# One more chunk pair on seven products in each feed-forward block of a decoder layer

## The chip, the cores and the metric

The kernel runs on one core of one Trainium2 chip. The metric is the device time of one execution in microseconds. A core has five engines, each with its own instruction queue that runs in order: TensorE (PE in the profile; its weight loads are PEld), VectorE (DVE), ScalarE (ACT), GpSimd (POOL) and SyncE (SP, which here only issues transfers). They meet through semaphores: an instruction that waits holds everything behind it on its engine. Weights come from device memory by DMA into on-chip memory (SBUF); matmul results go to accumulation banks (PSUM), of which this kernel uses eight, three named `acc`, three `mm` and two `tr`.

## What is computed

One decoder layer on 256 tokens of width 2048, in float32: a feed-forward (SwiGLU, inner width 5632), a mixer of sliding-window attention and a gated linear recurrence, cross-attention into a fixed memory, a second feed-forward, and a last norm. Cut to what matters here:

```python
def rms_norm(x, g):
    y = x * lax.rsqrt(jnp.mean(x * x, axis=-1, keepdims=True) + NORM_EPS)
    return y * g

def swiglu(h, w_gate, w_up, w_down):
    return (jax.nn.silu(h @ w_gate) * (h @ w_up)) @ w_down

x = x + 0.5 * swiglu(rms_norm(x, ffn1_norm), ffn1_w_gate, ffn1_w_up, ffn1_w_down)
x = gated_parallel_mixer(x, ...)
x = memory_cross_attention(x, mem, ...)
x = x + 0.5 * swiglu(rms_norm(x, ffn2_norm), ffn2_w_gate, ffn2_w_up, ffn2_w_down)
return rms_norm(x, final_norm)
```

## The kernel before

**Precision.** Every large operand is kept as two parts, hi (a rounded copy, made by ScalarE) and lo (operand less hi, made by VectorE). A product of a 128-row chunk of x with a 128 x 512 piece of weights is then three matmuls that add up in one bank: hi by hi, hi by lo, lo by hi (`times`, lines 397 to 399). For weights, `split_unit` makes hi (line 324) and lo (line 325) of two chunks at a time, 128 x 1024 numbers. hi and lo have three buffers each, so a split waits until TensorE is done with the piece three splits back.

**Feed-forward.** The inner width is cut into eleven column blocks j of 512, in groups of 4, 4 and 3. A block needs x by gate and x by up for both halves t of the tokens (128 each) over all sixteen chunks of x. After a group the product with the down weights follows. Block j = 0 takes plain products, gate and then up (`product`). The other ten (`product_pair`) go over eight chunk pairs q, 0 to 7. A plain pair takes eight products of a chunk (gate and up, two halves, two chunks), 24 matmuls. A pair in `SEVEN` takes seven, 21 matmuls, by the scheme of fast 2 x 2 matrix multiplication: with p1 to p7 from sums of x and sums of weights, all four results come out of seven products. For the sums of weights, `sums` adds four 128 x 512 pieces on VectorE (lines 335 to 338) into two tiles, ta and tb, and splits them into thi (line 340) and tlo (line 341), which have one buffer. For the sums of x, `combinations` makes, once for each feed-forward, four combinations for a pair in `SEVEN`, and two for a plain pair ahead of the last pair in `SEVEN` (`EARLY`); the adds run on GpSimd (lines 423 to 435), the cast chi on ScalarE (438) and clo on VectorE (439). Partial results stay in banks: p1, p3 and p5 in mm, p2 and p4 in acc, p6 and p7 in the two tr banks until the last pair in `SEVEN`, where VectorE folds them together (lines 497 to 501). From then on p2 to p5 collect the four results, which lines 513 to 521 turn into silu(gate) * up at the block's end.

Each block's result hb is transposed on TensorE through the tr banks (`feat`, line 534) and split into h (lines 539, 540) for the down product. These steps are a background generator, `transposed`, advanced by ticks between products.

**Weights.** In the feed-forwards a transfer brings 1 MB, four chunks of one weight ("wide", tile raw2, four buffers); a buffer comes free when VectorE has made the last lo from it. The second feed-forward's first four transfers still are of the narrow kind (tile raw). The wide tiles lie in the pool f2, whose memory the mixer's pool used before; the first transfer into each waits for the mixer's last use of that memory.

**Order.** The program text gives an order of issue; on each engine the final order is made by the framework's scheduler, from its own estimates. Work put in the order ahead of something late holds all behind it.

**Start of the second feed-forward.** `combinations` starts with the feed-forward; its adds, casts and splits run beside block j = 0, whose Silu is at line 607. GpSimd also brings x back from device memory there (line 1360).

Of the kernel before, what the change touches and what calls it, by code (L numbers as in the profile page):

```python
# [34 lines left out]
AHEAD, LOADED = 2, 4  # L35


SEVEN = (1, 3)
EARLY = tuple(q for q in range(max(SEVEN)) if q not in SEVEN)


# [87 lines left out]
def decoder_layer(ctx: ExitStack, tc: tile.TileContext, a: dict, out: bass.AP):  # L129
# [276 lines left out]
                k + i == 0, k + i == nk - 1,  # L406
            )

    def combinations(sp, x: Act):


        n = 4 * len(SEVEN) + 2 * len(EARLY)
        parts = [sp.tile([P, n, P], F32R, tag="c" + e, name="c" + e) for e in ("hi", "lo")]
        c = {"parts": parts, "at": {}, "done": False}

        def work():
            o = 0
            for q in range(max(SEVEN) + 1):
                while not {2 * q, 2 * q + 1} <= x.done:
                    yield  # L420
                v = sp.tile([P, 2, 2, P], F32, tag="u", name="u", bufs=2)
                f = sp.tile([P, 4, P], F32, tag="u", name="u", bufs=2)
                pool.tensor_tensor(
                    v[:].rearrange("p k t n -> p k (t n)"), f32(x.at(0, 2 * q, 2)),
                    f32(x.at(1, 2 * q, 2)), ALU.add,
                )
                if q in SEVEN:
                    n = 4
                    pool.tensor_tensor(f[:, 0], v[:, 0, 1], v[:, 1, 1], ALU.add)
                    pool.tensor_tensor(f[:, 1], f[:, 0], v[:, 0, 0], ALU.subtract)  # L430
                    pool.tensor_tensor(f[:, 2], v[:, 0, 0], v[:, 0, 1], ALU.subtract)
                    pool.tensor_tensor(f[:, 3], v[:, 1, 0], f[:, 1], ALU.subtract)
                else:
                    n = 2
                    pool.tensor_tensor(f[:, :2], v[:, :, 0], v[:, :, 1], ALU.subtract)
                yield from idle(3)
                s = slice(o, o + n)
                act.copy(parts[0][:, s], f[:, :n])
                dve.tensor_tensor(parts[1][:, s], f[:, :n], f32(parts[0][:, s]), ALU.subtract)
                c["at"][q] = o  # L440
                o += n
                yield
            c["done"] = True

        bg.spawn("mem", work())
        return c

    def product_pair(sp, x: Act, c, r, w):

        pw, _, nk, _, n = plan[at["product"]]
        assert pw[0].tensor is w.tensor
        at["product"] += 1
        b, begun = {}, set()
        hb = sp.tile([P, 2, 512], F32, tag="hb", name="hb", bufs=2)
        u2, u3 = (sp.tile([P, 512], F32, tag="u", name="u", bufs=2) for _ in range(2))
        late = nk // KU - 1  # L460

        def add(to, x_, w_, last):
            if to not in b:
                b[to] = {"p1": mm, "p3": mm, "p5": mm, "p2": acc, "p4": acc}.get(to, tr)()
            times(
                b[to][:], x_, w_, to not in begun, last, skip_group_check=True,
            )
            begun.add(to)

        def of_x(t, k):  # L470
            return [x.at(p, k)[:, t * P : (t + 1) * P] for p in range(2)]

        def of_c(q, i):
            return [p[:, c["at"][q] + i, :] for p in c["parts"]]

        def of_w(parts_, i):
            return [p[:, i, :] for p in parts_]

        for q in range(nk // KU):
            k = KU * q  # L480
            last = q == late
            if q in SEVEN:
                bg.until(lambda: c["done"])
                g, u, s = next_item()
                end = q == max(SEVEN)
                seven = (
                    ("p1", of_x(0, k), of_w(g, 0), end), ("p2", of_x(0, k + 1), of_w(g, 1), False),
                    ("p3", of_c(q, 3), of_w(u, 1), False), ("p5", of_c(q, 0), of_w(s, 0), end),
                    ("p7", of_c(q, 2), of_w(s, 1), end), ("p6", of_c(q, 1), of_w(s, 2), end),
                    ("p4", of_x(1, k + 1), of_w(s, 3), False),  # L490
                )
                for i, p in enumerate(seven):
                    add(*p)
                    if i % 2:
                        bg.tick()
                    if end and i == 1:
                        act.copy(hb[:, 0], b["p1"][:])
                if end:
                    dve.tensor_tensor(u2[:], b["p6"][:], hb[:, 0], ALU.add)
                    dve.tensor_tensor(u3[:], b["p7"][:], u2[:], ALU.add)  # L500
                    dve.tensor_tensor(u2[:], b["p5"][:], u2[:], ALU.add)
                continue
            g, u = next_item()
            for to, t, wt in (("p2", 0, g), ("p4", 1, g), ("p3", 0, u), ("p5", 1, u)):
                for i in range(KU):
                    off = to == "p3" and q in EARLY
                    add(
                        to, of_c(q, i) if off else of_x(t, k + i), of_w(wt, i),
                        last and i == KU - 1,
                    )  # L510
                if last:
                    if to == "p2":
                        dve.tensor_tensor(hb[:, 0], b["p2"][:], hb[:, 0], ALU.add)
                        act.activation(hb[:, 0], hb[:, 0], AF.Silu, scale=r[0])
                    elif to == "p4":
                        dve.tensor_tensor(hb[:, 1], b["p4"][:], u3[:], ALU.add)
                        act.activation(hb[:, 1], hb[:, 1], AF.Silu, scale=r[1])
                    else:
                        t, v = (0, u2) if to == "p3" else (1, u3)
                        dve.tensor_tensor(v[:], b[to][:], v[:], ALU.add)  # L520
                        dve.scalar_tensor_tensor(
                            hb[:, t], v[:], r[t], hb[:, t], ALU.mult, ALU.mult
                        )
                bg.tick()
        return hb
# [18 lines left out]
    class Norm:  # L544
        def __init__(self, gain, x=None):
            self.gain = gain
            self.ss = stat.tile([P, 2, 4], F32, tag="ss", name="ss")
            self.x = x or Act(
                [xtp.tile([P, KD, T], F32R, tag="xhi", name="xhi")],
                [xtp.tile([P, KD, T], F32R, tag="xlo", name="xlo")], KD,  # L550
            )
# [32 lines left out]


    def feed_forward(sp, x, norm: Norm, wg, wu, wd, done, begin_last=lambda: None, last=False):
        c = combinations(sp, norm.x)
        for gi, (j0, nj) in enumerate(GROUPS):
            h = Act(
                [sp.tile([P, 16, T], F32R, tag="hhi", name="hhi")],  # L590
                [sp.tile([P, 16, T], F32R, tag="hlo", name="hlo")], 16,
            )

            def transposed(hb, c):
                for q in range(2):
                    split(h, c + 2 * q, 2, feat(hb, [2 * q * P, (2 * q + 1) * P]))
                    yield

            for j in range(j0, j0 + nj):
                if j > 0:  # L600
                    hb = product_pair(sp, norm.x, c, norm.r, wg)
                    bg.spawn("feat", transposed(hb, 4 * (j - j0)))
                    continue
                pg = product(norm.x, wg)
                hb = sp.tile([P, 2, 512], F32, tag="hb", name="hb", bufs=2)
                for t in range(2):
                    act.activation(hb[:, t, :], pg[t][:], AF.Silu, scale=norm.r[t])
                pu = product(norm.x, wu)
                for t in range(2):
                    dve.scalar_tensor_tensor(  # L610
                        hb[:, t, :], pu[t][:], norm.r[t], hb[:, t, :], ALU.mult, ALU.mult
                    )
                bg.spawn("feat", transposed(hb, 4 * (j - j0)))
            if gi == len(GROUPS) - 1:
                begin_last()
            for n in range(4):
                end = gi == len(GROUPS) - 1
                pd = product(h, wd, skew=last and end and n == 3)
                for t in range(2):
                    xs = x[:, t, n * 512 : (n + 1) * 512]  # L620
                    dve.scalar_tensor_tensor(xs, pd[t][:], 0.5, xs, ALU.mult, ALU.add)
                if end:
                    done(n)
# [796 lines left out]
```

## Time and profile before

| | |
|---|---|
| three runs, median (lowest to highest) | 2307.45 us (2306.52 to 2311.22) |
| the profiled execution, its time | 2307.24 us |
| its span on the core, mean granted TensorE clock | 2305.5 us, 0.997 |
| first feed-forward, from first matmul to last column block's down product | about 8 to 740 us |
| second feed-forward | about 1573 to 2300 us |
| copy of p1 to copy of p1 in neighbouring blocks | 43.18 us |
| DMA, mean rate over the span | 188 GB/s |

A row of the profile names engine, source line, operation, output and inputs, shape and count, then busy time and mean duration; the idle time before it and what ended that stand last. Durations of neighbouring matmuls overlap, so what a matmul costs is read from the distance between the starts. In the table of stretches the columns are busy time and count by engine (PE, PEld, DVE, ACT, POOL), granted clock, share of DMA and GB/s.

### The profile page before, as it was taken

The page shows a single profiled execution, that of the slowest core. Times are in us where ns is not written, and L with a number is a line of the kernel's source. Part 1 is how long each engine was busy: PE and PEld are TensorE (multiplying, and loading weights), DVE is VectorE, ACT ScalarE, POOL GpSimd, SP SyncE. Part 2 cuts the span into 40 slices and gives each one's busy share as a digit, 9 for nine tenths or more (in the row PEclk, how much of TensorE's full clock was granted, in tenths as well). Part 3 has the DMA queues.
Part 4 walks back from the last instruction along what each step waited for, and adds up shares of the span by engine and source line. Part 5 has one row for each costly group of instructions (what it writes and reads, how often), then busy time and mean ns, then how long its engine had stood idle before and what let it go on. Part 6 is the DMA issues. An engine that isn't in the chain of part 4 may idle for free.

```text
span 2305.5 us, 27706 instructions
## 1 busy us (share of the span) xinstructions
PE 2279.0 (99%) x10751; PEld 1867.7 (81%) x10751; DVE 1511.0 (66%) x1784; ACT 1143.8 (50%) x1534; POOL 159.1 (7%) x221
## 2 busy tenths in 40 slices
PE   9999999999999999999999999998999999999998
PEld 7888888888888877778888888887888888888886
DVE  6875677657865477895444466556875677756865
ACT  6544445434545467444344446555554454534544
POOL 4000000000000000201220030003000000000001
PEclk9999999999999999999999999999999999999999
DMA  7555565565564544676423576647565565555553
GB/s 252 188 200 190 193 201 194 190 199 192 201 233 143 163 139 138 193 227 210 141 85 101 166 262 224 191 164 245 183 207 195 183 205 197 197 187 201 200 201 128
DMA packets 219236, 432.73 MB, mean 188 GB/s; under 512 B 14139, under 2 KB 16416, under 8 KB 219104
## 3 DMA queue, kind: packets, MB, share of 16 engines
q1 hardware_dynamic: 210432, 404.78, 52.7%
q0 software_dynamic: 8208, 25.39, 3.4%
q8 instruction: 84, 1.38, 0.2%
q10 hardware_dynamic: 464, 0.79, 0.1%
q14 instruction: 48, 0.39, 0.0%
HBM read 417.56 MB, written 13.11 MB: 187 GB/s over the span
## 4 chain that ended last, share of the span: by engine, by line
PE 90%; issue 4%; DVE 2%; ACT 1%; DMA 1%; POOL 1%; SPq 0%; POOLq 0%; ACTq 0%; DVEq 0%
PE acc L397 21%; PE acc L398 21%; PE acc L399 21%; PE mm L399 6%; PE mm L397 6%; PE mm L398 6%; PE tr L534 2%; PE mm L1119 1%; PE tr L399 1%; PE tr L397 1%; PE tr L398 1%; DVE lo L325 1%; PE tr L1088 1%; ACT s L762 0%; ACT hi L324 0%
## 5 line engine op out<-in xcount | busy, mean ns | idle before, releaser
L325 DVE TENSOR_TENSOR lo<-raw,hi 128x1024 fp32r<-128x1024 f32 (+1 forms) x770 | 918.3, 1198 | 652.3 <-ACT hi L324 648.4
L324 ACT CAST hi<-raw 128x1024 fp32r<-128x1024 f32 (+1 forms) x770 | 784.4, 1025 | 930.1 <-PE acc L399 713.5
L397 PE MATMUL acc<-hi,xhi 128*128 128x512 f32 (+1 forms) x1256 | 500.1, 399 | 7.8 <-ACT hi L324 2.9
L398 PE MATMUL acc<-lo,xhi 128*128 128x512 f32 (+1 forms) x1256 | 491.6, 391 | 3.5 <-DVE lo L325 3.4
L399 PE MATMUL acc<-hi,xlo 128*128 128x512 f32 (+1 forms) x1256 | 490.3, 391 | 1.2 <-DVE xlo L561 1.2
L397 PEld LDWEIGHTS acc<-hi,xhi 128*128 128x128 f32 x1256 | 236.5, 188 | 60.6 <-issue 5.1
L398 PEld LDWEIGHTS acc<-lo,xhi 128*128 128x128 f32 x1256 | 237.0, 189 | 53.7 <-DVE lo L325 5.5
L399 PEld LDWEIGHTS acc<-hi,xlo 128*128 128x128 f32 x1256 | 236.5, 188 | 50.3 <-DVE xlo L561 2.5
L397 PE MATMUL acc<-hi,hhi 128*128 128x512 f32 x704 | 275.0, 391 | 0.0
L399 PE MATMUL acc<-hi,hlo 128*128 128x512 f32 x704 | 274.6, 390 | 0.0
L398 PE MATMUL acc<-lo,hhi 128*128 128x512 f32 x704 | 274.6, 390 | 0.0
L398 PE MATMUL mm<-lo,xhi 128*128 128x512 f32 x440 | 171.2, 389 | 0.0
L399 PE MATMUL mm<-hi,xlo 128*128 128x512 f32 x440 | 171.2, 389 | 0.0
L397 PE MATMUL mm<-hi,xhi 128*128 128x512 f32 x440 | 171.2, 389 | 0.0
L398 PEld LDWEIGHTS acc<-lo,hhi 128*128 128x128 f32 x704 | 132.2, 188 | 27.1
L399 PEld LDWEIGHTS acc<-hi,hlo 128*128 128x128 f32 x704 | 132.2, 188 | 26.9
L397 PEld LDWEIGHTS acc<-hi,hhi 128*128 128x128 f32 x704 | 132.2, 188 | 26.8
L341 DVE TENSOR_TENSOR tlo<-raw,thi 128x1024 fp32r<-128x1024 f32 x80 | 95.9, 1219 | 19.9 <-ACT thi L340 19.9
L398 PEld LDWEIGHTS mm<-lo,xhi 128*128 128x128 f32 x440 | 82.6, 188 | 17.3
L397 PEld LDWEIGHTS mm<-hi,xhi 128*128 128x128 f32 x440 | 82.6, 188 | 17.2
L399 PEld LDWEIGHTS mm<-hi,xlo 128*128 128x128 f32 x440 | 82.6, 188 | 17.2
L340 ACT CAST thi<-raw 128x1024 fp32r<-128x1024 f32 x80 | 82.0, 1050 | 28.1 <-PE acc L399 27.9
(347 smaller groups left out, 2618.2 us busy)
## 6 DMA issues: line engine op xcount, KB each, us to landing
raw<-in_ffn_w_up_dram SPq DMA_DIRECT2D x88, 1024.0 KB, 5.1
raw<-in_ffn_w_down_dram SPq DMA_DIRECT2D x88, 1024.0 KB, 5.1
raw<-in_ffn_w_gate_dram SPq DMA_DIRECT2D x84, 1024.0 KB, 5.1
raw<-in_w_in_dram SPq DMA_DIRECT2D x136, 512.0 KB, 3.5
raw<-in_w_out_dram SPq DMA_DIRECT2D x32, 512.0 KB, 4.7
raw<-in_w_proj_attn_dram SPq DMA_DIRECT2D x16, 512.0 KB, 3.5
raw<-in_w_proj_rwkv_dram SPq DMA_DIRECT2D x16, 512.0 KB, 6.4
raw<-in_w_cross_kv_dram SPq DMA_DIRECT2D x16, 512.0 KB, 3.6
```

What stands on the lines that cost most here:

```text
L324: act.copy(hi[:, s], raw[:, s])
L325: dve.tensor_tensor(lo[:, s], raw[:, s], f32(hi[:, s]), ALU.subtract)
L340: act.copy(hi[:, 2 * i : 2 * i + 2], t[:])
L341: dve.tensor_tensor(lo[:, 2 * i : 2 * i + 2], t[:], f32(hi[:, 2 * i : 2 * i + 2]), ALU.subtract)
L397: pe.matmul(o, xh, hi, start=first, stop=False, **how)
L398: pe.matmul(o, xh, lo, start=False, stop=False, **how)
L399: pe.matmul(o, xl, hi, start=False, stop=last, **how)
L534: pe.transpose(b[:, o : o + P], tok[:, t, col : col + P], ident[:])
L1088: pe.matmul(b[e][:, m * P : (m + 1) * P], x1[r, j, cs_], x2[r, j, cs_], start=True, stop=True,)
L1119: pe.matmul(vb[:, o : o + P][:, r], lhs(e), rhs[:, r], start=first and e == 0, stop=True, **ek,)
```

## The change

Three edits, and what follows from them:

- `SEVEN` goes from pairs 1 and 3 to pairs 0, 2 and 4, so three of eight pairs take seven products; `EARLY` becomes 1 and 3. In a seven pair p3 and p5 move to the end.
- The sums of x are formed by VectorE in place of GpSimd, and wait until the norm's factor r has been issued.
- In the second feed-forward the tiles hhi, hlo, hb, thi and tlo are asked for first, so the wide raw weights come to lie behind them, at other addresses.
- As p6 and p7 now hold the tr banks from a block's first pair on, a block's transposes are started after the next block's last seven pair; those of a group's last block at once.

```diff
-SEVEN = (1, 3)
+SEVEN = (0, 2, 4)
 EARLY = tuple(q for q in range(max(SEVEN)) if q not in SEVEN)
...
-    def combinations(sp, x: Act):
+    def combinations(sp, norm):
-        n = 4 * len(SEVEN) + 2 * len(EARLY)
+        x, n = norm.x, 4 * len(SEVEN) + 2 * len(EARLY)
...
-        c = {"parts": parts, "at": {}, "done": False}
+        c = {"parts": parts, "at": {}, "done": False, "next": []}
         def work():
             o = 0
+            while norm.r is None:
+                yield
             for q in range(max(SEVEN) + 1):
-                while not {2 * q, 2 * q + 1} <= x.done:
-                    yield
...
-                pool.tensor_tensor(
+                dve.tensor_tensor(
                     v[:].rearrange("p k t n -> p k (t n)"), f32(x.at(0, 2 * q, 2)),
                     f32(x.at(1, 2 * q, 2)), ALU.add,
                 )
                 if q in SEVEN:
                     n = 4
-                    pool.tensor_tensor(f[:, 0], v[:, 0, 1], v[:, 1, 1], ALU.add)
+                    dve.tensor_tensor(f[:, 0], v[:, 0, 1], v[:, 1, 1], ALU.add)
...
-                yield from idle(3)
+                yield
                 s = slice(o, o + n)
                 act.copy(parts[0][:, s], f[:, :n])
+                yield
                 dve.tensor_tensor(parts[1][:, s], f[:, :n], f32(parts[0][:, s]), ALU.subtract)
...
                     ("p1", of_x(0, k), of_w(g, 0), end), ("p2", of_x(0, k + 1), of_w(g, 1), False),
-                    ("p3", of_c(q, 3), of_w(u, 1), False), ("p5", of_c(q, 0), of_w(s, 0), end),
                     ("p7", of_c(q, 2), of_w(s, 1), end), ("p6", of_c(q, 1), of_w(s, 2), end),
                     ("p4", of_x(1, k + 1), of_w(s, 3), False),
+                    ("p3", of_c(q, 3), of_w(u, 1), False), ("p5", of_c(q, 0), of_w(s, 0), end),
...
                     dve.tensor_tensor(u2[:], b["p5"][:], u2[:], ALU.add)
+                    while c["next"]:
+                        bg.spawn("feat", c["next"].pop())
...
     def feed_forward(sp, x, norm: Norm, wg, wu, wd, done, begin_last=lambda: None, last=False):
-        c = combinations(sp, norm.x)
+        if last:
+            for tag, shape, dt, bufs in (
+                ("hhi", [P, 16, T], F32R, 1), ("hlo", [P, 16, T], F32R, 1),
+                ("hb", [P, 2, 512], F32, 2), ("thi", [P, 4, 512], F32R, 1),
+                ("tlo", [P, 4, 512], F32R, 1),
+            ):
+                sp.tile(shape, dt, tag=tag, name=tag, bufs=bufs)
+        c = combinations(sp, norm)
...
                     hb = product_pair(sp, norm.x, c, norm.r, wg)
-                    bg.spawn("feat", transposed(hb, 4 * (j - j0)))
+
+                    c["next"].append(transposed(hb, 4 * (j - j0)))
+                    if j == j0 + nj - 1:
+                        bg.spawn("feat", c["next"].pop())
```

In the changed file the lines behind the edits stand 1 to 14 lower: L513 to L521 become L516 to L524, the transposes L534 become L537, their split L539 and L540 become L542 and L543, the Silu of block 0 L607 becomes L621.

More of the change, by code (lines that the diff above doesn't have):

```diff
@@ L428, in work @@
                     n = 4
-                    pool.tensor_tensor(f[:, 0], v[:, 0, 1], v[:, 1, 1], ALU.add)
-                    pool.tensor_tensor(f[:, 1], f[:, 0], v[:, 0, 0], ALU.subtract)
-                    pool.tensor_tensor(f[:, 2], v[:, 0, 0], v[:, 0, 1], ALU.subtract)
-                    pool.tensor_tensor(f[:, 3], v[:, 1, 0], f[:, 1], ALU.subtract)
+                    dve.tensor_tensor(f[:, 0], v[:, 0, 1], v[:, 1, 1], ALU.add)
+                    dve.tensor_tensor(f[:, 1], f[:, 0], v[:, 0, 0], ALU.subtract)
+                    dve.tensor_tensor(f[:, 2], v[:, 0, 0], v[:, 0, 1], ALU.subtract)
+                    dve.tensor_tensor(f[:, 3], v[:, 1, 0], f[:, 1], ALU.subtract)
                 else:
                     n = 2
-                    pool.tensor_tensor(f[:, :2], v[:, :, 0], v[:, :, 1], ALU.subtract)
-                yield from idle(3)
+                    dve.tensor_tensor(f[:, :2], v[:, :, 0], v[:, :, 1], ALU.subtract)
+                yield
                 s = slice(o, o + n)
                 act.copy(parts[0][:, s], f[:, :n])
+                yield
                 dve.tensor_tensor(parts[1][:, s], f[:, :n], f32(parts[0][:, s]), ALU.subtract)
@@ L546, in __init__ @@
             self.gain = gain
+            self.r = None
             self.ss = stat.tile([P, 2, 4], F32, tag="ss", name="ss")
```

## The prediction

> **What bounds the kernel now.** I read the page first, then TensorE's waits by stretches, then one column block of a feed-forward, then the start of the second feed-forward, where the waits lie.
>
> From the page, engines and the chain that ended last:
>
> ```profile
> PE 2279.0 (99%) x10751; PEld 1867.7 (81%) x10751; DVE 1511.0 (66%) x1784; ACT 1143.8 (50%) x1534; POOL 159.1 (7%) x221
> PE 90%; issue 4%; DVE 2%; ACT 1%; DMA 1%; POOL 1%; SPq 0%; POOLq 0%; ACTq 0%; DVEq 0%
> ```
>
> TensorE is busy almost throughout and holds nine tenths of the chain; a busy TensorE could still be slow, so its waits matter. In the stretch from 30 to 740 us, nearly all of the first feed-forward, the view of waits lists none. From 1575 us to the end it lists three, all at the start of the second feed-forward:
>
> ```profile
> PE acc L397 <- ACT hb L607: 2.5, 1, 2.5
> PE acc L397 <- ACT hi L324: 2.1, 1, 2.1
> PE acc L398 <- DVE lo L325: 1.3, 1, 1.3
> ```
>
> So the blocks are paced by the number of matmuls. Their pitch, from TensorE's timeline over one plain chunk pair (24 matmuls, from the first acc product of the last pair to the first of the next block):
>
> ```profile
> 140.22 0.39 PE L397 MATMUL acc<-hi,xhi 128*128 128x512 f32 x1
> ...
> 145.66 0.39 PE L397 MATMUL acc<-hi,xhi 128*128 128x512 f32 x1
> ```
>
> (145.66 - 140.22) / 24 = 0.2267 us; the 0.39 beside each row is latency, which overlaps. One block runs from 120.30 to 163.48 us, copy of p1 (L497) to copy of p1; busy time by engine in that stretch:
>
> ```profile
> 120.30:163.48 43.18, 43.18 (x196) 35.51 (x195) 34.30 (x39) 22.35 (x26) 0.00 (x0) 1.00 0.57 194
> ```
>
> VectorE (third figure) has 34.30 us of work in 43.18, TensorE's clock is full, DMA is at 0.57.
>
> **Part 1, one more pair of seven products.** A pair is 8 products of 3 matmuls as a plain pair and 7 as a seven pair. Blocks j > 0 number 10 in each feed-forward (4+4+3 blocks less the first), 20 in all. Each loses 3 matmuls: 20 x 3 x 0.2267 = 13.6 us off the path, if nothing new holds TensorE. Transposes, evictions and weight bytes are unchanged.
>
> The price lies on VectorE and ScalarE. Pitches on VectorE, in this block:
>
> ```profile
> 134.49 0.69 DVE L335 TENSOR_TENSOR raw<-raw,raw 128x512 f32<-128x512 f32 x1
> 135.10 0.69 DVE L336 TENSOR_TENSOR raw<-raw 128x512 f32<-128x512 f32 x1
> ...
> 138.04 1.22 DVE L341 TENSOR_TENSOR tlo<-raw,thi 128x1024 fp32r<-128x1024 f32 x1
> 139.18 1.22 DVE L325 TENSOR_TENSOR lo<-raw,hi 128x1024 fp32r<-128x1024 f32 x1
> ...
> 145.41 1.28 DVE L520 TENSOR_TENSOR u<-mm,u 128x512 f32<-128x512 f32 x2
> 146.61 1.40 DVE L521 SCALAR_TENSOR_TENSOR hb<-u,rs,hb 128x512 f32<-128x512 f32 x2
> 147.94 1.22 DVE L325 TENSOR_TENSOR lo<-raw,hi 128x1024 fp32r<-128x1024 f32 x1
> ```
>
> 512 columns start 0.61 after one another, 1024 columns 1.14. A further seven pair adds four sums (2.4) and two tlo (2.3) and halves one lo (-0.5): 4.1 us a block, so 38.4 of 42.5 us (43.18 - 0.68), 90%. ScalarE gains two casts and loses half of one, 22.35 + 1.6 = 24, no bound. Since VectorE runs in order, 90% needs a walk. Count from the end of a block; pairs q0 to q4 take 4.76, 5.44, 4.76, 5.44, 4.76, so they begin at 0, 4.76, 10.2, 15.0, 20.4 and q5 at 25.2. Before, the first lo behind the block's last products starts 147.94 - 145.66 = 2.28 after its end. The changed order puts one sum (L335, 0.6) ahead of it: it ends at 2.28 + 0.6 + 1.2 = 4.1, and q1 needs it at 4.76: 0.65 to spare, the least of all. Behind it: q1's other lo 5.2, two sums 6.4, q2's lo 7.5, last sum 8.1, tlo 9.2 and 10.4. The new product order (p1, p2, then p7, p6) asks for these at 10.2, 11.6 and 12.2. q3's lo waits for a hi buffer that q1 frees at 10.2: 10.2 + 1.05 (ScalarE) + 1.2 = 12.5 against 15.0; q4's tlo 18.3 and 19.4 against 21.8 and 22.4; q5's lo 22.7 against 25.2. The sums of the next q0 stand some 10 us before the seam. p3 and p5 moved to the end of a seven pair, so their banks are wanted at 3.4 and 4.1 after the seam, while VectorE has read the old ones by 145.41 + 1.28 - 145.66 = 1.0, and by 1.7 with a 0.7 us product of the gate (half of the L521 row) that the changed order puts between. Hence I cost the 4.1 us at nothing: TensorE's own 42.5 us cover it. Without cover it would be 4.1 x 20 = 82 us; I keep 0 to 3 us for the range, because every deadline of the walk is met.
>
> The row and a rule disagree here. The Trainium skill, "VectorE: DVE Perf Modes", section "The DRAIN you can't avoid", says that the next VectorE operation doesn't start until the pipeline has emptied. The rows above start 0.61 apart at a duration of 0.69. By the rule, the block's 39 + 5 operations would be 0.08 longer each, 38.4 + 3.5 = 41.9 of 42.5, and the walk's 0.65 would shrink to about 0.2: the time stays, but I would give the seam rival below twice its chance. The trace disagrees with the rule, so I take the rows.
>
> **Part 2, sums of x on VectorE, and their place.** Twice a run five pairs need sums. VectorE takes on 5 adds of 512 columns (0.6), 12 of 128 and 2 of 256, and one more clo (0.6). The trace has no 128-column add of this kind alone on VectorE: between 0.1 (nothing but a quarter of 0.61 less its start) and 0.29 (center, L211, at 4.22 us); I take 0.2, nearest to L211's shape: 3.0 + 2.4 + 0.7 + 0.6 = 6.7 us a feed-forward, in the first block's 43 us, where VectorE has that room.
>
> What it removes shows at the start of the second feed-forward. ScalarE, in order, and TensorE:
>
> ```profile
> 1583.33 0.40 ACT L438 CAST chi<-u 128x256 fp32r<-128x256 f32 x1 [4.28 <-POOL u L435]
> 1599.01 0.62 ACT L438 CAST chi<-u 128x512 fp32r<-128x512 f32 x1 [3.98 <-POOL u L432]
> 1600.60 1.28 ACT L607 ACT_TABLE_LOAD   x1
> ```
> ```profile
> 1582.29 0.39 PE L399 MATMUL acc<-hi,xlo 128*128 128x512 f32 x1
> 1584.73 0.73 PE L397 MATMUL acc<-hi,xhi 128*128 128x512 f32 x2 [2.06 <-ACT hi L324]
> 1586.75 0.80 PE L398 MATMUL acc<-lo,xhi 128*128 128x512 f32 x1 [1.29 <-DVE lo L325]
> ...
> 1602.64 0.50 PE L397 MATMUL acc<-hi,xhi 128*128 128x512 f32 x1 [2.49 <-ACT hb L607]
> ```
>
> The casts of the sums wait for GpSimd, and the weight casts and the Silu (L607) stand behind them. The second stall costs 1602.64 - 1599.98 = 2.66, and ten matmuls at half clock after it (1602.64 to 1606.59) cost 3.95 - 2.27 = 1.7: 4.3 us. In the changed order the last cast waits for VectorE, which finishes the sums about 1593 (from 1579.1: the walk below plus seven more weight splits). The gate product ends near 1598, table load and Silu of its first half by 1599.0, and the bank is wanted at 1599.6: gone, 4.3 us gained. The first stall stays, a little shorter: VectorE starts at 1579.1 (end of the norm's squares), and before the first weight split stand four 512 adds (2.4), eight 128 adds (1.6), two clo (0.9), one 256 add and the reduce (0.5): 1584.5; the split ends at 1585.7, before at 1586.7. I take 0.8 gained, for hand-offs; bounds -1 to 2. Sum 5.1.
>
> **Part 3, place of the raw weights.** The first wide load is issued at 1570.91 now, behind the last product of cross-attention; in the changed program it waits only for the recurrence's old gate tiles, so it goes right behind the load issued at 1563.61. It landed at 1575.9 and its cast came at 1583.6, so it wasn't what was late: 0.
>
> **Part 4, transposes put off.** p7 and p6 now hold both tr banks from q0 to q4, so transposes wait until q4 is read; only those of the first block (j = 0) fall into the next block's q0, where p6 waits for their cast (0.58) and lo (0.68) behind three other products (2.0): between 0 and 0.5 us in each feed-forward, by how much VectorE has queued; I take the middle, +0.5 in all. The start of the first feed-forward, paced by the first weights and x, I leave at 0 (-1 to 1).
>
> Sum against the profiled execution's 2307.24 us (span 2305.5 and 1.7 around it, 0.2 under the median of 2307.45): 2307.24 - 13.6 - 5.1 + 0.5 = 2289.0.
>
> **The rivals.**
> - Half cure: VectorE's 6.7 us merely takes GpSimd's place, and the Silu is late again. For it: the first weight split still stands behind 5.4 us of sums. Against: only GpSimd's 2.16 us adds made 1599. Time 2307.2 - 13.6 = 2293.6.
> - Seam late: hand-offs eat the 0.65 us and 0.4 more in each block. For it: 90% on an in-order engine. Against: no wait at 79% now. 2289 + 20 x 0.4 = 2297.
> - Slower: the next q0's two tlo (2.3 us) slip into the seam, if ScalarE's thi comes late behind weight casts. Each block then loses 2.3 - 0.65 = 1.63 us: 2289 + 32.6 = 2322. It decides from 0.91 us a block (18.2 / 20). Against: thi is free from 25.2, seventeen us earlier.
> - The saved matmuls are eaten exactly: seam late by 0.7 to 1.1 us beyond the slack, 2303 to 2311.
>
> **How the numbers follow.** Forecast 0.70, half cure 0.12, seam 0.08, eaten 0.04, slower 0.06. Changes under 0.2% (4.6 us) can't be told from none. Faster (below 2302.8): 0.90; same 0.04; slower 0.06. The range takes in forecast, half cure and seam: low 2289 - 2 (first split, start) - 2 = 2285, high 2297.
>
> **What would show it.** Right: blocks 42.5 us apart from p1 copy to p1 copy, no wait of TensorE between 30 and 730 us, 60 fewer 512-column matmuls, one stall at the start of the second feed-forward and none by the Silu. Wrong: waits of TensorE for lo or tlo in every block, above all at its second pair; a gap before a Silu's table load.

## The result, and the profile after

The changed kernel takes 2288.89 us (median of four runs, 2287.26 to 2290.31), the kernel before 2308.75 beside it: ratio 0.9914, 95% interval 0.9901 to 0.9927. The forecast was 2289.0, range 2285 to 2297. The profiled execution took 2288.73 us, span 2287.0.

Engines and the chain that ended last, from the page of the changed kernel:

```profile
PE 2263.7 (99%) x10691; PEld 1857.0 (81%) x10691; DVE 1600.3 (70%) x1944; ACT 1181.2 (52%) x1576; POOL 132.1 (6%) x193
PE 89%; issue 4%; DVE 4%; ACT 2%; DMA 2%; SPq 0%; POOL 0%; POOLq 0%; ACTq 0%; DVEq 0%
```

TensorE has 60 matmuls fewer (10751 before) and VectorE 89 us more work (1511.0 before); the chain is still TensorE's. The block that ran from 120.30 to 163.48 us before is best compared with an ordinary one of the second group of blocks, from copy of p1 to copy of p1, in the view by stretches (busy time and count of PE, PEld, DVE, ACT, POOL):

```profile
337.14:379.58 42.44, 42.44 (x193) 35.15 (x192) 38.37 (x45) 24.32 (x28) 0.00 (x0) 1.00 0.58 198
```

42.44 us for 43.18, with VectorE at 38.37. TensorE's waits, the first feed-forward (30 to 740 us) first, then from 1575 us to the end:

```profile
PE tr L537 <- DVE hb L624: 0.2, 1, 0.2
...
PE acc L398 <- DVE lo L325: 2.5, 2, 1.9
PE acc L397 <- ACT hi L324: 1.5, 1, 1.5
```

The wait for hb at the Silu (2.49 us before) is not among them. The waits for hi and lo at the start of the second feed-forward are still there.

Where the span's 18.5 us came from, by the gaps between starts of neighbouring matmuls beyond the pitch of 0.2267 us (this counts stretches in which the granted clock is 0.5, too): 13.6 are the 60 matmuls; the start of the second feed-forward lost 9.5 and now 5.5 (+4.0); the start of the first lost 5.9 and now 4.1 (+1.8); the blocks of the two feed-forwards have new gaps of 0.9 and 1.2 (-2.1); the mixer in between is 0.6 shorter. The sum is 17.9; the rest is spread over gaps too small for this count (under 0.1 us).

### The profile page after: what moved, and what is told of

Same layout as the page of the kernel before. It is cut to its first block, busy times and chain, and to the rows that moved or that the text cites. A ratio compares the mean times of both kernels' runs of the same rounds, so it can differ in the third digit from the quotient of the medians.

```text
span 2287.0 us, 27787 instructions
## 1 busy us (share of the span) xinstructions
PE 2263.7 (99%) x10691; PEld 1857.0 (81%) x10691; DVE 1600.3 (70%) x1944; ACT 1181.2 (52%) x1576; POOL 132.1 (6%) x193
## 4 chain that ended last, share of the span: by engine, by line
PE 89%; issue 4%; DVE 4%; ACT 2%; DMA 2%; SPq 0%; POOL 0%; POOLq 0%; ACTq 0%; DVEq 0%
PE acc L397 20%; PE acc L398 20%; PE acc L399 20%; PE mm L399 6%; PE mm L398 6%; PE mm L397 6%; PE tr L537 2%; DVE lo L325 1%; PE mm L1133 1%; PE tr L398 1%; PE tr L399 1%; PE tr L397 1%; PE tr L1102 1%; DMA raw<-in_ffn_w_up_dram 1%; ACT hi L324 1%
## 5 line engine op out<-in xcount | busy, mean ns | idle before, releaser
L397 PE MATMUL acc<-hi,xhi 128*128 128x512 f32 (+1 forms) x1196 | 477.1, 399 | 4.8 <-ACT xhi L564 2.7
L398 PE MATMUL acc<-lo,xhi 128*128 128x512 f32 (+1 forms) x1196 | 466.8, 390 | 4.4 <-DVE lo L325 4.3
L399 PE MATMUL acc<-hi,xlo 128*128 128x512 f32 (+1 forms) x1196 | 465.2, 389 | 0.0
L398 PEld LDWEIGHTS acc<-lo,xhi 128*128 128x128 f32 x1196 | 225.3, 188 | 53.4 <-DVE lo L325 7.7
L399 PEld LDWEIGHTS acc<-hi,xlo 128*128 128x128 f32 x1196 | 224.8, 188 | 47.4 <-issue 1.0
L340 ACT CAST thi<-raw 128x1024 fp32r<-128x1024 f32 x120 | 125.5, 1052 | 73.4 <-DVE raw L336 37.3
L397 PE MATMUL mm<-hi,xhi 128*128 128x512 f32 x380 | 149.1, 392 | 0.0
L399 PE MATMUL mm<-hi,xlo 128*128 128x512 f32 x380 | 148.1, 390 | 0.0
L398 PE MATMUL mm<-lo,xhi 128*128 128x512 f32 x380 | 148.1, 390 | 0.0
L341 DVE TENSOR_TENSOR tlo<-raw,thi 128x1024 fp32r<-128x1024 f32 x120 | 145.1, 1220 | 0.0
```

What stands on the lines that cost most here:

```text
L340: act.copy(hi[:, 2 * i : 2 * i + 2], t[:])
L341: dve.tensor_tensor(lo[:, 2 * i : 2 * i + 2], t[:], f32(hi[:, 2 * i : 2 * i + 2]), ALU.subtract)
L397: pe.matmul(o, xh, hi, start=first, stop=False, **how)
L398: pe.matmul(o, xh, lo, start=False, stop=False, **how)
L399: pe.matmul(o, xl, hi, start=False, stop=last, **how)
```

## The experiments

Each is compared with the kernel before on the same chip, and ratios are compared with the 0.9914 of the changed kernel; the time under each is its own median.

Beside the ratio stands the time that both feed-forwards take together in the profiled execution: the first from its first product to the last matmul of its down product, the second from the last matmul of cross-attention to TensorE's last. It is 1452.2 us in the kernel before (726.0 and 726.2) and 1434.2 in the changed kernel (718.1 and 716.1). What lies between them, the mixer and cross-attention, takes 835.9 us in the changed kernel and up to 841.1 in other runs, though no edit here touches it.

### How much the third pair is worth

```diff
-SEVEN = (0, 2, 4)
+SEVEN = (1, 3)
```

> The changed kernel with the seven products in pairs 1 and 3 only; all else as changed. Theory (the third pair's 60 matmuls come off the path whole, VectorE's 4.1 us a block are covered): 60 x 0.2267 = 13.6 us come back, 2288.9 + 13.6 = 2302.5 us, p1 copies 43.1 us apart, VectorE near 1520 us busy. Rival (part of the third pair's gain is eaten by VectorE, and the starts of the feed-forwards gave more than I read): 8 us or less come back, 2297 us or below.

Measured: 2301.85 us, ratio 0.9963 (0.9949 to 0.9976), so 11.3 us over the changed kernel's ratio; the profiled span is 2300.1, 13.1 over 2287.0, but 1.8 of that lie in the mixer. The feed-forwards take 1445.6 us, 11.3 more. Ordinary blocks are 43.11 us apart. So the third pair is worth 11.3 us net: its 60 matmuls are 13.6, and the new gaps of 0.9 and 1.2 us in the blocks, which this run doesn't have, take most of the difference. The rival's 8 us or less would be a ratio of 0.995, at the edge of the interval, and the spacing of the blocks speaks against it.

### Sums of x back on GpSimd

```diff
-            while norm.r is None:
-                yield
             for q in range(max(SEVEN) + 1):
+                while not {2 * q, 2 * q + 1} <= x.done:
+                    yield
...
-                dve.tensor_tensor(
+                pool.tensor_tensor(
```

(and so for the other sums; the turns between them as before the change)

> The changed kernel with the sums of x formed on GpSimd again, each pair as soon as its x is there, as before the change. Theory (GpSimd's sums hold the casts and with them the Silu): the wait of TensorE for hb behind the Silu is back at the start of the second feed-forward, and what that start gained (4.1 us) is lost again, with GpSimd's one further pair of sums (2 us) on top at most: 2293 to 2295 us. Rival (the start gained from the place of the raw weights): 2289 us, no wait for hb.

Measured: 2300.01 us (2296.14 to 2303.23), ratio 0.9953 (0.9940 to 0.9965), 9 us over the changed kernel, and 7.7 in the profiled spans, 7.0 of them in the feed-forwards (1441.2 us): more than expected. ScalarE's timeline of this kernel, the casts of the sums with the idle time before them and what ended it, and TensorE's at the Silu:

```profile
1578.07 0.62 ACT L438 CAST chi<-u 128x512 fp32r<-128x512 f32 x1 [4.64 <-POOL u L432]
...
1587.62 0.62 ACT L438 CAST chi<-u 128x512 fp32r<-128x512 f32 x1 [3.96 <-POOL u L432]
...
1595.77 0.62 ACT L438 CAST chi<-u 128x512 fp32r<-128x512 f32 x1 [3.13 <-POOL u L432]
```
```profile
1579.68 0.73 PE L397 MATMUL acc<-hi,xhi 128*128 128x512 f32 x2 [2.63 <-ACT hi L324]
1581.74 0.80 PE L398 MATMUL acc<-lo,xhi 128*128 128x512 f32 x1 [1.32 <-DVE lo L325]
1599.39 0.50 PE L397 MATMUL acc<-hi,xhi 128*128 128x512 f32 x1 [2.90 <-ACT hb L620]
```

The Silu's stall is back with GpSimd, as the theory says, though the place of the raw weights is that of the changed kernel: the rival falls. By gaps the start of the second feed-forward loses 10.3 us against 5.5. What I had not expected is the first feed-forward: its first 50 us lose 6.1 here, 5.9 before the change, and 3.1 to 4.4 in every run with the sums on VectorE. TensorE waits there for xlo, a split that VectorE makes: once here, 1.0 us, three times before the change, 1.6 us together, and in no run with the sums on VectorE. Here it also waits 1.4 us for hb at the first Silu. So the sums on GpSimd cost at both starts.

### Without the place of the raw weights

```diff
-        if last:
-            for tag, shape, dt, bufs in (
-                ("hhi", [P, 16, T], F32R, 1), ("hlo", [P, 16, T], F32R, 1),
...
-                sp.tile(shape, dt, tag=tag, name=tag, bufs=bufs)
```

> The changed kernel without the block of tiles that sets the place of the raw weights in the second feed-forward. Theory (the weights were not what was late): 2288.9 us, within 1 us; the wide loads of that feed-forward are issued 6 us later again, right behind the last product of cross-attention. Rival (the earlier loads carry part of the gain at the start): 2291 to 2293 us, with a wait of TensorE for hi or lo longer by as much.

Measured: 2291.23 us, ratio 0.9919 (0.9905 to 0.9932); span 2288.8, feed-forwards 1434.2 us as in the changed kernel. TensorE's waits at the start are the same, hi 1.5 and lo 1.9. But the edit didn't do what the theory says of it. The first wide load is issued 6.1 us ahead of the last matmul of cross-attention here, 6.2 ahead in the changed kernel and 0.5 behind it in the kernel before: the early loads come without this block of tiles too. So the run doesn't test what early loads are worth, every run here has them, and the rival stays open.

### Sums later, by turns alone

```diff
+            yield from idle(later)        # 8 in the second feed-forward
             for q in range(max(SEVEN) + 1):
```

> The changed kernel with the sums of x in the second feed-forward begun 8 turns (4 chunk pairs) later. Theory (what is left at that start, 5.5 us lost with its half clock, is the first weight splits standing behind 6.4 us of sums on VectorE and the casts behind them on ScalarE): the waits for hi L324 and lo L325 near 1574 to 1578 us go, 2288.9 - 5.5 = 2283.4 us; down to 2286 if the last squares of the norm still hold ScalarE. Rival (the weights or the norm are what is late there): 2288.9 us, same waits.

Measured: 2290.55 us, ratio 0.9914 (0.9901 to 0.9928), same waits. That looks like the rival, but the run tested nothing: from the norm's last reduction on, the instructions stand on VectorE in the same order as in the changed kernel. The framework's scheduler (the planner, below) didn't follow the turns in the program. The next run forces the order.

### Sums behind the weight splits

```diff
-            dve.tensor_tensor(lo[:, s], raw[:, s], f32(hi[:, s]), ALU.subtract)
+            at["lo"] = dve.tensor_tensor(lo[:, s], raw[:, s], f32(hi[:, s]), ALU.subtract)
...
+            yield from idle(later)        # 8 in the second feed-forward
...
+                with tc.issue_after(at["lo"].ins) if later else nullcontext():
-                dve.tensor_tensor(
+                    dve.tensor_tensor(
                         v[:].rearrange("p k t n -> p k (t n)"), f32(x.at(0, 2 * q, 2)),
```

> The changed kernel with each sum of x in the second feed-forward put behind the newest weight split on VectorE, by an explicit edge of order, and begun 8 turns later. In the run with the 8 turns alone the order on VectorE did not change at all, since a planner sets it by what it holds ready, so it tested nothing. Theory (the waits at that start are weight splits behind 6.4 us of sums): here three splits stand ahead of the first sum, the waits for hi L324 and lo L325 near 1574 to 1578 us go and with them the half clock; 2288.9 - 5.5 = 2283.4 us beside a kernel before of 2308.75, ratio 0.989. Rival (the weights or the norm are what is late there): ratio 0.9914 as for the changed kernel, same waits.

Measured: 2284.01 us, ratio 0.9894 (0.9877 to 0.9910), span 2282.3. First the changed kernel's start of the second feed-forward: VectorE (some of its sums, one per row), ScalarE, TensorE.

```profile
1570.73 0.68 DVE L423 TENSOR_TENSOR u<-xhi,xlo 128x512 f32<-128x512 f32 x1
...
1571.66 0.28 DVE L431 TENSOR_TENSOR u<-u 128x128 f32<-128x128 f32 x1
1571.86 0.28 DVE L430 TENSOR_TENSOR u<-u 128x128 f32<-128x128 f32 x1
1572.18 0.29 DVE L432 TENSOR_TENSOR u<-u 128x128 f32<-128x128 f32 x1
1572.50 0.69 DVE L423 TENSOR_TENSOR u<-xhi,xlo 128x512 f32<-128x512 f32 x1
...
1576.45 0.69 DVE L423 TENSOR_TENSOR u<-xhi,xlo 128x512 f32<-128x512 f32 x1
1577.06 2.35 DVE L325 TENSOR_TENSOR lo<-raw,hi 128x1024 fp32r<-128x1024 f32 x2
```
```profile
1570.43 0.19 ACT L573 ACTIVATION_READ_ACCUMULATOR junk<-x 128x1 f32 x1
1572.50 0.62 ACT L438 CAST chi<-u 128x512 fp32r<-128x512 f32 x1 [1.88 <-DVE u L432]
1574.34 0.40 ACT L438 CAST chi<-u 128x256 fp32r<-128x256 f32 x1 [1.22 <-DVE u L435]
1574.65 1.99 ACT L324 CAST hi<-raw 128x1024 fp32r<-128x1024 f32 x2
```
```profile
1575.74 0.73 PE L397 MATMUL acc<-hi,xhi 128*128 128x512 f32 x2 [1.49 <-ACT hi L324]
1578.34 0.50 PE L398 MATMUL acc<-lo,xhi 128*128 128x512 f32 x1 [1.86 <-DVE lo L325]
```

ScalarE ends the norm at 1570.6 and then sits idle for 1.88 and 1.22 us, for sums, with the weight cast that TensorE needs next behind them. VectorE has 6.4 us of sums (1570.65 to 1577.06) ahead of its first split. Then the same two engines, ScalarE and VectorE, in this run:

```profile
1570.53 0.19 ACT L575 ACTIVATION_READ_ACCUMULATOR junk<-x 128x1 f32 x1
1570.62 2.10 ACT L324 CAST hi<-raw 128x1024 fp32r<-128x1024 f32 x2
```
```profile
1570.94 0.17 DVE L586 TENSOR_SCALAR ms<-ms 128x2 f32<-128x2 f32 x1
1571.69 2.36 DVE L325 TENSOR_TENSOR lo<-raw,hi 128x1024 fp32r<-128x1024 f32 x2 [0.57 <-ACT hi L324]
```

The cast follows the norm at once, the split comes 5.4 us earlier, and TensorE loses nothing between 1550 and 1600 us. The theory holds: weights and norm were in time, the sums were in the way. The 5.5 us of gaps there are gone; the ratio fell by 0.0020, 4.6 us, with intervals that just overlap, and the feed-forwards take 1428.5 us, 5.7 less (two runs below repeat it).

### VectorE's cover: more sums

The line once more, and in the second run twice more; the output doesn't change.

```diff
         dve.tensor_tensor(ta[:, 0], ru[:, 0], rg[:, 0], ALU.subtract)
+        dve.tensor_tensor(ta[:, 0], ru[:, 0], rg[:, 0], ALU.subtract)
```

> The changed kernel with the first sum of weights of every seven pair (L335) formed twice: 3 x 0.6 = 1.8 us more VectorE work a block, 40.2 of 42.5 us (95%), 36 us over the 20 blocks. Theory (the third pair's VectorE work lies in cover, and cover is left): 0 to 2 us, ratio 0.991 to 0.993. Rival (at 90% the in-order engine is at its edge, hand-offs at the seam have eaten the slack of 0.6 us): 0.6 to 1.8 us a block, 12 to 36 us, ratio 0.997 to 1.007, with waits of TensorE for lo L325 in every block.

> The same sum formed three times: 3.6 us more VectorE work a block, 42.0 of 42.5 us (99%). Theory (the cover is TensorE's own time, but the walk's least slack is 0.65 us at the seam and VectorE can't catch up before it at 99%): some 0.5 to 1.2 us lost a block, 10 to 24 us, ratio 0.996 to 1.002. Rival A (only the sum over the block counts): ratio 0.9914. Rival B (no cover at all): 3.6 x 20 = 72 us, ratio 1.023.

Measured: 2299.09 us, ratio 0.9959 (0.9943 to 0.9975), for the sum formed twice; 2300.36 us, ratio 0.9966 (0.9953 to 0.9979), formed thrice. So some 10 and 12 us lost, hardly more for twice the extra work. The feed-forwards take 1442.7 and 1444.9 us, 8.5 and 10.7 more than in the changed kernel. In each, 3.4 us more at the granted clock 0.5, at the start of a feed-forward, cost 1.7 of that; what is left is 0.35 and 0.45 us a block. The other 5 us of the first run's span (2300.5) lie in the mixer: the granted clock is 0.5 there for 6.8 us from 803.7 and for 3.4 from 984.6, and half of this time is the 5.1 us that the mixer is longer. The profile doesn't tell why the clock fell there.

In the blocks of the first run TensorE loses most where p7 and p6 take up tlo, 4.1 us and another 2.8 at the matmuls right behind; at lo it loses 0.7 (0.9 in the changed kernel). In the second run these three are 2.5, 2.7 and 3.5. So my theory of free cover (0 to 2 us) falls, but the rival isn't right either: its 12 us or more were to come from lo in every block, and what comes late first is tlo. For the sum formed thrice the forecast total of 10 to 24 us holds, at its lower end.

### The same load in one place

```diff
                 bg.tick()
+        for _ in range(3):
+            dve.tensor_tensor(junk_t[:], hb[:, 0], hb[:, 1], ALU.add)
         return hb
```

> The changed kernel with three additions of 512 columns that nobody reads, right behind each block's tail: 1.8 us more of VectorE a block, as in the run with the first sum formed twice, which lost some 10 us, but in one place, behind the first weight split of the block's second pair, where the trace of the changed kernel shows 2.2 us to spare up to the next use. Theory (the place decides, not the load): 0 to 3 us, ratio 0.991 to 0.993. Rival (95% load on VectorE costs wherever it is put): 10 us again, ratio 0.995 or 0.996.

Measured: 2301.64 us, ratio 0.9968 (0.9957 to 0.9979): 12 us lost. The feed-forwards take 1445.1 us, 10.8 more, of which 6.8 us more at the granted clock 0.5 cost 3.4; what is left is 0.4 us a block. First the changed kernel's VectorE behind a seam between two blocks (p1 of the new block starts at 357.97):

```profile
361.13 2.35 DVE L325 TENSOR_TENSOR lo<-raw,hi 128x1024 fp32r<-128x1024 f32 x2
363.40 0.68 DVE L336 TENSOR_TENSOR raw<-raw 128x512 f32<-128x512 f32 x1
364.01 0.68 DVE L337 TENSOR_TENSOR raw<-raw,raw 128x512 f32<-128x512 f32 x1
364.61 1.22 DVE L325 TENSOR_TENSOR lo<-raw,hi 128x1024 fp32r<-128x1024 f32 x1
365.74 0.68 DVE L338 TENSOR_TENSOR raw<-raw,raw 128x512 f32<-128x512 f32 x1
366.35 2.43 DVE L341 TENSOR_TENSOR tlo<-raw,thi 128x1024 fp32r<-128x1024 f32 x2
368.69 2.05 DVE L325 TENSOR_TENSOR lo<-raw,hi 128x512 fp32r<-128x512 f32 x2
```

The first tlo is done at 367.6, and p7 takes it up at 369.76: 2.2 us to spare. But the second is done at 368.78, and p6 takes it up at 370.44: 1.7 to spare, less than the 1.8 that the edit adds. Then this run, the same place (its seam is 2.4 us later), and the matmuls of p7 and then p6 on TensorE:

```profile
368.03 0.68 DVE L529 TENSOR_TENSOR junk<-hb 128x512 bf16<-128x512 f32 x1
368.64 0.68 DVE L336 TENSOR_TENSOR raw<-raw 128x512 f32<-128x512 f32 x1
369.24 0.68 DVE L337 TENSOR_TENSOR raw<-raw,raw 128x512 f32<-128x512 f32 x1
369.84 0.68 DVE L325 TENSOR_TENSOR lo<-raw,hi 128x512 fp32r<-128x512 f32 x1
370.44 0.68 DVE L338 TENSOR_TENSOR raw<-raw,raw 128x512 f32<-128x512 f32 x1
371.05 2.43 DVE L341 TENSOR_TENSOR tlo<-raw,thi 128x1024 fp32r<-128x1024 f32 x2
```
```profile
371.91 0.39 PE L397 MATMUL tr<-thi,chi 128*128 128x512 f32 x1
372.31 0.50 PE L398 MATMUL tr<-tlo,chi 128*128 128x512 f32 x1
372.65 0.40 PE L399 MATMUL tr<-thi,clo 128*128 128x512 f32 x1
372.89 0.40 PE L397 MATMUL tr<-thi,chi 128*128 128x512 f32 x1
373.53 0.50 PE L398 MATMUL tr<-tlo,chi 128*128 128x512 f32 x1 [0.23 <-DVE tlo L341]
```

The planner, with another order to fill, also put the half split (lo 128x512, 0.6 us) ahead of the last sum (L338), where it stood behind both tlo before. Counted from the block's start, tlo comes 2.3 us later, against 2.2 and 1.7 to spare: p7 waits a little (0.40 from start to start for a pitch of 0.23) and p6 more (0.64). So the run doesn't decide between place and load: the slack that it was to fill was smaller than I had read it, at one use in one block. Over the 20 blocks of the changed kernel p6 of pair 2 has from 0.05 to 3.7 us to spare, less than 1.8 in ten. Adding up what these ten lack gives 7.6 us, an estimate of what 1.8 us at this place would cost in the old order; 7.4 were lost. The half split stands ahead of the last sum in 24 of 60 seven pairs here, in 24 with the first sum formed twice, in 2 with it formed thrice, and in none of the changed kernel. How much of the loss comes from this move and how much from the 1.8 us isn't separated.

### A fourth pair

```diff
-SEVEN = (0, 2, 4)
+SEVEN = (0, 1, 2, 3)
```

> The changed kernel with seven products in pairs 0, 1, 2 and 3 (as many sums of x kept as with 0, 2 and 4): 60 matmuls fewer again, 41.8 us of TensorE a block, and VectorE 38.4 + 4.1 = 42.5 us. Theory (VectorE paces the block now): no gain over three pairs, ratio 0.991 at the best; four seven pairs in a row ask 25.6 us of VectorE against 19.0 us of TensorE, and a lead of two pairs carries at most some 5 us, so rather 1 to 2 us a block lost, ratio 0.995 to 1.005, with waits for lo and tlo. Rival (the number of matmuls still decides): 2288.9 - 13.6 = 2275.3 us, ratio 0.9855.

Measured: 2322.38 us, ratio 1.0070 (1.0047 to 1.0093), above the theory's upper end of 1.005 and far from the rival. A block by stretches, copy of p1 to copy of p1, and TensorE's largest wait over the run:

```profile
379.56:424.83 45.27, 43.21 (x189) 34.04 (x188) 42.44 (x52) 25.70 (x29) 0.00 (x0) 1.00 0.56 190
```
```profile
PE tr L397 <- ACT thi L340: 28.5, 30, 2.0
```

VectorE has its 42.4 us of work and the block takes 45.3, so the number of matmuls no longer decides. But VectorE is idle for 2.8 us of the block, and the theory's cause, that VectorE paces it, isn't what the trace shows. Here is one of the 30 waits: the sum on VectorE, TensorE's last matmul that reads the old thi and its wait for the new one, and the cast on ScalarE between them:

```profile
378.17 0.68 DVE L336 TENSOR_TENSOR raw<-raw 128x512 f32<-128x512 f32 x1
```
```profile
379.11 0.39 PE L399 MATMUL acc<-thi,xlo 128*128 128x512 f32 x1
380.68 0.50 PE L397 MATMUL tr<-thi,chi 128*128 128x512 f32 x1 [0.73 <-ACT thi L340]
```
```profile
379.58 1.05 ACT L340 CAST thi<-raw 128x1024 fp32r<-128x1024 f32 x1
```

The sum is ready at 378.85. The cast starts 0.7 us later, 0.08 after TensorE's last matmul with the pair before has ended: thi has one buffer, and TensorE waits for a tile that it held itself. In 23 of the 30 waits, 20.5 of the 28.5 us, it is TensorE that releases the cast, when the sums have been ready for 0.4 to 1.1 us. With a plain pair between two seven pairs, in the changed kernel, no wait for thi is listed; with four in a row there is no time for the cast. Whether VectorE's load would be the next limit, with two buffers of thi and tlo, wasn't tried.

### Order of the seven products

```diff
-                    ("p7", ...), ("p6", ...),
-                    ("p4", ...),
                     ("p3", ...), ("p5", ...),
+                    ("p7", ...), ("p6", ...),
+                    ("p4", ...),
```

> The changed kernel with the seven products of a pair in their order of before (p1, p2, p3, p5, p7, p6, p4). Theory (banks and sums have time in either order): p3 and p5 want their banks 1.4 and 2.0 us after a block's start, VectorE has read the old ones by -0.2 and 1.3; the first use of tlo is one product later; ratio 0.991 as for the changed kernel, within 0.0015. Rival (the new order is needed since p5's bank is late): 0.3 us or more a block, 6 us, ratio 0.994 or above, with waits of TensorE's mm products for VectorE's u.

> The sums of the second feed-forward behind the weight splits, as in the run that gave ratio 0.9894, and the seven products in their order of before. Theory (the order of the products has time either way): ratio 0.9894, within 0.0015. Rival (the later first use of tlo takes away the last waits in the blocks, 0.9 and 1.6 us in the two feed-forwards): ratio 0.988.

Measured: 2291.45 us, ratio 0.9933 (0.9916 to 0.9950), for the old order in the changed kernel, and 2284.57 us, ratio 0.9901 (0.9886 to 0.9916), with the sums behind the splits. Against 0.9914 and 0.9894 both are a little higher. The intervals overlap with those of the runs that they are compared with, and the first ratio is outside the band that I gave. Its profiled span is 2287.9, and from 1590 us on TensorE's waits list nothing; in the second run one wait for a bank, of 0.6 us, is listed. The feed-forwards take 1434.1 us in the first run, for 1434.2, and 1429.2 in the second, for 1428.5. So the traces show no effect of the order, and the rival's 0.3 us a block, 6 us, is not there.

### The sums behind the splits, a little earlier

The edit of the run with ratio 0.9894, and:

```diff
-        c = combinations(sp, norm, 8 if last else 0)
+        c = combinations(sp, norm, 4 if last else 0)
```

> The sums of x in the second feed-forward behind the newest weight split as in the run that gave ratio 0.9894, but begun 4 turns later and not 8: one split stands ahead of the first sum, and the sums end earlier. Theory (one split ahead is enough for the start, and the wait for lo near 1655 us, 0.9 us, came from sums that ran late): no wait of TensorE between 1560 and 1700 us, 2283.1 us beside a kernel before of 2308.75, ratio 0.9885 to 0.9895. Rival (the waits at the start come back in part since the later splits alternate with sums): ratio 0.990 to 0.9914, waits for lo L325 near 1575 us.

Measured: 2284.75 us, ratio 0.9905 (0.9888 to 0.9921), span 2281.9. The ratio lies in the rival's band, but the rival's waits at the start aren't there; the wait for lo near 1655 us is unchanged, 0.7, so late sums are not its cause, and that part of the theory falls. The three runs with the sums behind the splits have medians of 2284.0, 2284.6 and 2284.8 us beside 2306.9 to 2307.8 for the kernel before: the best version here, by the ratios 2 to 5 us below the changed kernel. Their feed-forwards take 1428.5, 1429.2 and 1429.0 us, 5.1 to 5.7 less than the changed kernel's, about the 5.5 that the gaps at that start had cost.

## Why the prediction was right

**The third pair (13.6 us).** Right in its reason, and in its size as a gross gain. 60 matmuls are gone and the pitch is unchanged; undoing the pair gives back 11.3 us in the feed-forwards, since the changed order brings 2.1 us of new gaps with it. "38.4 of 42.5 us" on VectorE is 38.37 of 42.44 in the trace. The walk's narrow place at the seam is there too: the first lo of the second pair ends at 362.3, 4.3 us after the block's start (4.1 predicted), and TensorE takes it up at 362.96, 5.0 after it (4.76 predicted, but it is the pair's second matmul that reads lo). So 0.65 to spare came out as 0.6 with both ends 0.2 later. It was clearly missed in one of 20 blocks, by 0.8 us behind the matmul at 1659.83. It isn't "the least of all", though: p6 of pair 2, for which the walk has 1.8 us (10.4 against 12.2), had less than 0.65 in four blocks.

**"Hence I cost the 4.1 us at nothing."** Right for this order of work, but the text made it sound safer than it is. It priced missing cover at 82 us, as if cover were there or not. The runs show an edge close by: 1.8 us more a block costs 0.35 to 0.4, and 3.6 more costs 0.45. The rival "seam late" (0.4 us a block) had the right size of cost, and it came with the next 1.8 us of work, but mostly at the use of tlo and not at the seam.

**Sums on VectorE (5.1 us, measured 4.0).** The Silu's stall is gone whole, as predicted: table load at 1589.37, Silu at 1590.66, no wait. The mis-sized term is the first stall, "I take 0.8 gained": by gaps it went from 5.2 to 5.5 us lost. The 5.4 us of sums ahead of the first split were 6.4: half of the difference is that dependent sums don't follow each other at 0.2, another 0.3 is the two clo, 1.2 for 0.9. And the weight's cast stood behind casts of sums on ScalarE, which the walk of VectorE alone had left out.

**Start of the first feed-forward ("leave at 0, -1 to 1").** Wrong: 1.8 us gained, past the bound. I had put that start down to weights and x alone, and left out that VectorE's split of x was late beside GpSimd's sums: 1.6 us of waits for xlo are gone, and the run with the sums on GpSimd has one of 1.0 again.

**Place of the raw weights (0), transposes (+0.5).** The early loads didn't shorten the first stall: the waits for hi and lo are there in the changed kernel with loads 6.2 us ahead. What the place is worth isn't tested, since the loads are as early without it. The transposes' wait shows once in each feed-forward, 0.68 us from start to start at 58.79 and 0.39 at 1613.64, where the pitch is 0.23: +0.6 in all. Undoing the deferral wasn't tried: p7 and p6 hold both `tr` banks in the first pair.

That the total of 2289.0 came out to 0.3 us is luck, since errors cancel: 1.1 too much expected at the second start and 1.6 of further gaps in the blocks, against 1.8 at the first start, 0.6 in the mixer and 0.6 that have no place.

## What to carry to other kernels

Count the matmuls that an edit removes and check each in-order helper engine for its tightest deadline, on every engine that a value passes: here ScalarE's casts decided a start that VectorE's walk alone got wrong. Take the slack as the least over all uses and all blocks; one use in one block overstated it, and an edit can move the order besides. Look at tiles with one buffer before blaming an engine's load. When side work and the data of the next matmul become ready together, force the order (data first) by an explicit edge. And check in the trace that an edit moved what it was to move: two edits here did not.

## What the runs showed of the hardware

A 128-column sum on VectorE starts 0.20 us after one that it doesn't depend on, though each lasts 0.28; after one that it needs it starts 0.32 later, just behind its end (1571.66 to 1571.86 and 1571.86 to 1572.18 above). The rule of the Trainium skill that I weighed, "VectorE: DVE Perf Modes", section "The DRAIN you can't avoid", thus fits the dependent pairs of this trace and not the independent ones; the same section of the Trainium skill adds that an operation that isn't held starts earlier, which the prediction left out.

With GpSimd forming the sums, VectorE's own work beside it stretches: the split of 512 columns (clo) took up to 1.83 us and 1.02 on average, 0.69 with GpSimd idle; that of 256 columns 1.06 on average, 0.42 with the sums on VectorE. From two groups, the first of the run with GpSimd, the second of the changed kernel:

```profile
L439 DVE TENSOR_TENSOR clo<-u,chi 128x256 fp32r<-128x256 f32 x4 | 4.2, 1059 | 1.3 <-ACT chi L438 1.3
```
```profile
L440 DVE TENSOR_TENSOR clo<-u,chi 128x256 fp32r<-128x256 f32 x4 | 1.7, 417 | 0.0
```

The Trainium skill, "SBUF — State Buffer", section "SBUF: two separate sides", says that VectorE with two inputs from SBUF and GpSimd take turns at one shared pair of ports, whole instructions at a time; the two rows agree with it. So the sums moved to VectorE cost that engine less than their own time: its busy time is 1600.3 us with them and 1594.3 without, and their rows add up to 15.4.
